# A decoder layer on one core: the first token gather reads two rounded parts of the normed rows, split by ScalarE and GpSimd

## The chip, the cores and the metric

One core of a Trainium2 chip runs the whole program. The time is that of the device for one execution, in microseconds (us); the metric is the median of several. Engines are called as the profile calls them: PE (TensorE, matmuls), PEld (its weight loads), DVE (VectorE), ACT (ScalarE), POOL (GpSimd) and SP (SyncE, which issues nearly all DMAs). "Granted clock" is the share of TensorE's 2.4 GHz that the chip lets through: 1.0 or 0.5 (1.2 GHz).

## The reference, cut to what matters

256 tokens of width 1024 pass one layer: a token mixing part (sparse attention, stick-breaking attention, output projections), a LayerNorm, a router and a mixture of 32 experts, of which each token uses 4. The part that matters here:

```
x  = post_norm(ALPHA * x + gate1 * y, ln1_g, ln1_b)        # 256 x 1024
h  = layer_norm(x) * (1 + scale2) + shift2
logits = h @ w_router + b_router;  top 4 of 32 -> gate
for each expert e: rows of h of its tokens -> gu -> clamped SwiGLU -> down, weighted, summed per token
x  = post_norm(ALPHA * x + gate2 * y, ln2_g, ln2_b)
```

All is float32. The weights of the experts are 384 MB of 2 MB blocks and are read once.

## The kernel before, in words

The 256 tokens lie on 128 partitions in two halves (`tt` is 0 or 1). The program has two parts: token mixing (about the first 256 us) and the experts (the rest). Between them lies a short chain around the router.

**The chain between the parts.** For each half, `normed(tt)` writes the new rows `x`, `logits(tt)` transposes them on PE and multiplies with the router's weights, and `stats2(tt)` takes mean and variance. `unit_rows(tt)` (line 900) writes `zz[:, tt, :]`, the normed rows without scale and shift, with one DVE instruction of 1024 columns. `choose(tt)` (lines 868 to 881) finds the four largest logits, `routed[:, tt, :]` (line 877), and counts on PE how many tokens with the same expert stand ahead (`pspos`). `place(tt)` makes `posm` (line 885) and from it the one-hot matrix `A0` (line 887), two DVE instructions per half, 64 columns each: column p of expert a is 1 where the token is the p-th of expert a. Two experts (`STATIC`) are handled first, with 64 places each, so `A0` is used in 128 columns. All these DVE instructions are pinned to their order in the program: `unit_rows(0)`, `choose(0)`, `unit_rows(1)`, `choose(1)`, `place(0)`, `place(1)`.

**The gather.** `gather(g, kp)` (lines 1083 to 1099) multiplies the normed rows, as stationary operand in blocks of 128x128, with the one-hot matrix of group `g`, as moving operand. The result `psg` is the transposed rows of the group's tokens; ACT applies scale and shift and writes `xt` (line 1098). Group 0 (the two first experts) uses the float32 rows `zz` and a float32 `A0`; the trace has two instructions for each float32 matmul. The later groups (7 of them) use two parts, `zzH` (the rows rounded to fp32r) and `zzL` (what is left), so two matmuls in fp32r. These parts are made by `split_rows` (lines 1279 to 1286): a copy on ACT and a subtraction on DVE for each half, queued on DVE behind the last instruction of `place`.

**The experts.** `plan` lists for each expert four blocks of `w_gu` and two of `w_dn`, 2 MB each. SP issues their loads into a ring of five buffers; a load waits until PE has finished with the block that was in the buffer (`xpump`). PE works in the order of the program: `mult_gu` starts with bias matmuls (`psu<-bgu`, line 1143), then 16 matmuls of 512 columns for each block (line 1149). `after` hangs small jobs behind blocks: `ranking` (the order of the other experts, from line 936 on) behind blocks 0 to 2, and so on.

**What sets the order.** A planner orders each engine's instructions by the program's order and by when its own model thinks them ready; `pin`, `behind` and `issue_after` hold chosen ones in place. Each engine then works strictly in its order.

Of the kernel before, what the change touches and what calls it, by code (L numbers as in the profile page):

```python
# [10 lines left out]
F32 = mybir.dt.float32  # L11
F32R = mybir.dt.float32r
# [7 lines left out]
D = 1024  # L20
# [40 lines left out]
def trunk_kernel(ctx: ExitStack, tc: tile.TileContext, i, out):  # L61
    nc = tc.nc
# [162 lines left out]
    sp = ctx.enter_context(tc.tile_pool(name="sp", bufs=1))  # L225
# [32 lines left out]
    def pin(ins, j=0):  # L258
        if j < 4:
            tc.keep_in_program_order(ins)  # L260
# [144 lines left out]
    biasT = sp.tile([128, HA, S], F32, name="biasT")  # L405
    nc.gpsimd.dma_start(biasT, bass.AP(tensor=fd.tensor, offset=fd.offset, ap=[[1, 128], [384, HA], [1, S]]))
    wukT = sp.tile([128, 4, 128], F32, name="wukT")
# [61 lines left out]
    late = {}  # L469
# [243 lines left out]
    n = 0  # L713
    while units[n][0] in cols:
        conv(n + LA)
        name = units[n][0]
# [63 lines left out]
    zz = sp.tile([128, 2, D], F32, name="zz", tag="gaT")  # L780
# [35 lines left out]
    n = n_mix  # L816
# [14 lines left out]
    m8s, lgs, anchor = [], [], []  # L831
# [3 lines left out]
    def normed(tt):  # L835
        z = zz[:, tt, :]
        residual(tt, 1)
        pin(zbn[tt, 1])
        mv, rs = finish_stats(wk, zst[tt], f"z{tt}", late=True)
        pin(nc.vector.scalar_tensor_tensor(z, z, mv[:, 0:1], l1g, op0=ALU.subtract, op1=ALU.mult))  # L840
        pin(nc.vector.reciprocal(rs, rs))
        pin(nc.vector.scalar_tensor_tensor(x[:, tt, :], z, rs, l1b, op0=ALU.mult, op1=ALU.add))

    def stats2(tt):
        st = wk.tile([128, 2, 6], F32, name=f"st_h{tt}", tag="st", bufs=4)
        for a in range(2):
            pin(nc.vector.bn_stats(st[:, a, :], x[:, tt, a * 512:(a + 1) * 512]))
        ln2[tt] = finish_stats(wk, st, f"h{tt}", late=True)
# [35 lines left out]
    def place(tt, ps):  # L884
        pin(nc.vector.scalar_tensor_tensor(posm[:, tt, :], ps, 1.0, routed[:, tt, :], op0=ALU.add, op1=ALU.mult))
        for a in range(STATIC):
            ins = nc.vector.tensor_scalar(A0[:, tt, a * 64:(a + 1) * 64], iota[:, :64], posm[:, tt, a:a + 1], None,
                                          op0=ALU.is_equal)
            pin(ins)
        return ins  # L890

    A0 = sp.tile([128, 2, 256], F32, name="A", tag="wukT")
    normed(0)
    logits(0)
    normed(1)
# [1 line left out]
    def unit_rows(tt):  # L897
        mv, rs = ln2[tt]
        pin(nc.vector.reciprocal(rs, rs))
        pin(nc.vector.tensor_scalar(zz[:, tt, :], x[:, tt, :], mv[:, 0:1], rs, op0=ALU.subtract, op1=ALU.mult))  # L900

    stats2(0)
    stats2(1)
    unit_rows(0)
    ps = choose(0)
    unit_rows(1)
    ps1 = choose(1)
    place(0, ps)
# [81 lines left out]
    def base_sums(pT4):  # L990
        for tt in range(2):
            for nh in range(2):
                ps = tp.tile([128, 512], F32, name="psbd")
                nc.tensor.matmul(ps, pT4[:, 2 + tt, :], bdn[:, nh * 512:(nh + 1) * 512], start=True, stop=True)
                nc.scalar.copy(acc[:, tt, nh * 512:(nh + 1) * 512], ps)
# [65 lines left out]
    for j in range(STATIC, E):  # L1061
# [5 lines left out]
        used += wide[j]  # L1067
    A, XT, SL, OT, AT, YS, P, PY, ACTV = {0: A0}, {}, {}, {}, {}, {}, {}, {}, {}

    def width(g):  # L1070
        return sum(wide[j] for j in groups[g])
# [10 lines left out]
    def gather(g, kp):  # L1082
        n = width(g)
        if kp == 0:
            XT[g] = sp.tile([128, 8, 256], F32, name="xt", tag="hL" if g % 2 else "qlT")
        ps = ms.tile([128, 2, 256], F32, name="psg")
        for q in range(2):
            k = 2 * kp + q
            ks = slice(k * 128, (k + 1) * 128)
            terms = [(z, tt) for z in ((zz,) if g == 0 else (late["zzH"], late["zzL"])) for tt in range(2)]  # L1090
            for m, (z, tt) in enumerate(terms):
                ins = nc.tensor.matmul(ps[:, q, :n], z[:, tt, ks], A[g][:, tt, :n], start=(m == 0),  # L1092
                                       stop=(m == len(terms) - 1))
                if g:
                    behind(ins, m)
        for q in range(2):
            k = 2 * kp + q
            nc.scalar.activation(XT[g][:, k, :n], ps[:, q, :n], AF.Identity, scale=mc[:, 1, k:k + 1],  # L1098
                                 bias=mc[:, 0, k:k + 1])

    def behind(ins, n):
        tc.keep_in_program_order(ins)

    def slots(j):
        g, c = gof[j]
        for t, m in enumerate(parts_of[j]):
            ps = ms.tile([128, 2], F32, name="pss")
            n = 0
            for tt in range(2):
                for h in range(128 // m):  # L1110
                    hot = A[g].bitcast(F32) if g else A[g]
                    behind(nc.tensor.matmul(ps[m * h:m * h + m, :], hot[:, tt, c + 64 * t:c + 64 * t + m],  # L1112
                                            rouR[:, tt, seq[j], :], start=(tt == 0), stop=(tt == 1),
                                            tile_position=(0, m * h)), n)
                    n += 1
            sl = wk.tile([128, 2], F32, name="sl", tag="slt", bufs=6)
            nc.vector.tensor_copy(sl, ps)  # L1117
            ot = wk.tile([128, S], F32R, name="ot", tag="pT", bufs=4)
            nc.vector.tensor_scalar(ot, iota, sl[:, 0:1], None, op0=ALU.is_equal)
            OT[j, t] = ot  # L1120
            SL[j, t] = sl
# [134 lines left out]
    for g in range(1, len(groups)):  # L1256
        n0 = at_unit[groups[g][0], 0, 0]
        job(max(n0 - 7, 1), one_hot, g)
        for kp in range(4):
            job(n0 - 6 + kp, gather, g, kp)  # L1260
        for j in groups[g]:
            job(at_unit[j, 0, 2], slots, j)
    for j in range(STATIC):
        job(at_unit[j, 0, 3] + 1, slots, j)
    for kp in range(4):
        gather(0, kp)
# [9 lines left out]
    def sorted_rows():  # L1276
        late["pT4"] = ranked()

    def split_rows():
        late["zzH"] = sp.tile([128, 2, D], F32R, name="zzH", tag="biasT")  # L1280
        late["zzL"] = sp.tile([128, 2, D], F32R, name="zzL")
        with tc.issue_after(anchor[2].ins):
            for tt in range(2):
                nc.scalar.copy(late["zzH"][:, tt, :], zz[:, tt, :])
                nc.vector.tensor_sub(late["zzL"][:, tt, :], zz[:, tt, :], late["zzH"][:, tt, :].bitcast(F32))

    acc = sp.tile([128, 2, D], F32, name="acc", tag="hH")
    for n, f in ((0, ranking), (1, ranking), (2, split_rows), (2, ranking), (3, sorted_rows),
                 (5, lambda: base_sums(late["pT4"]))):
        after.setdefault(n, []).insert(0, (f, ()))  # L1290
    xpump()
# [116 lines left out]
```

## Time and profile before

| | |
|---|---|
| median of 3 runs | 1219.64 us (1218.18 to 1220.34) |
| the profiled execution | 1221.51 us, of it 1219.7 us span of instructions |
| busy in the span | PE 86%, PEld 39%, DVE 35%, ACT 19%, POOL 4% |
| mean granted clock | 0.937 |
| DMA | 451.95 MB, 371 GB/s on the mean, 424 GB/s in most slices after 335 us |

The profile is one execution. A time in its timeline counts from the first instruction. Busy shares are means over stages with different limits; the change touches some 15 us around 270 us, so the rows further down are from there, and from places where the same kinds of instructions stand.

### The profile page before, as it was taken

To read this page: it belongs to the slowest core of one execution; us is meant where nothing else is said; L and a number is where in the kernel's file an instruction comes from. 1 tells how busy PE (TensorE), PEld (TensorE's weight loads), DVE (VectorE), ACT (ScalarE), POOL (GpSimd) and SP (SyncE) were. 2 spreads that over 40 slices of the span, in tenths; PEclk is the share of its full clock that TensorE was granted. 3 is DMA by queue.
4 is the path that set the end of the run, shared out by engine and by line. 5 is a ranking of instruction groups with operands and counts; after the bars stand their busy time and mean duration, and the time that the engine had idled before them with its cause. 6 is when DMAs were issued, how large, how long until landed. Compare 5 with 4: busy or idle time off the path is not lost.

```text
span 1219.7 us, 15731 instructions
## 1 busy us (share of the span) xinstructions
PE 1049.6 (86%) x6505; PEld 475.9 (39%) x6505; DVE 421.0 (35%) x810; ACT 233.7 (19%) x435; POOL 46.1 (4%) x93
## 2 busy tenths in 40 slices
PE   5997999989989889988989897989797979779764
PEld 5885878873323232333323222232123213322211
DVE  7788976782112121212121212121212211112234
ACT  2546655431200110011010101020001000100001
POOL 2140201000000000000000000000000000000001
PEclk9998999979999998999899998999899989999886
DMA  9956657377899999999999999999999999979993
GB/s 363 341 200 253 247 207 292 139 271 291 335 424 407 422 424 425 417 424 424 425 417 423 424 425 425 426 425 425 425 425 425 424 425 425 425 313 416 425 423 148
DMA packets 96270, 451.95 MB, mean 371 GB/s; under 512 B 5342, under 2 KB 6558, under 8 KB 64450
## 3 DMA queue, kind: packets, MB, share of 16 engines
q1 hardware_dynamic: 95442, 449.42, 90.5%
q0 software_dynamic: 752, 1.47, 0.4%
q8 instruction: 53, 0.87, 0.3%
q14 instruction: 23, 0.19, 0.0%
HBM read 461.98 MB, written 1.47 MB: 380 GB/s over the span
## 4 chain that ended last, share of the span: by engine, by line
issue 78%; PE 13%; DVE 6%; POOL 1%; ACT 0%; DMA 0%; SPq 0%; POOLq 0%; DVEq 0%; ACTq 0%
PE psp L430 4%; PE psn L449 2%; PE psy L797 2%; PE psbr L767 2%; DVE ada L290 1%; DVE ada L267 1%; DVE WL L214 1%; PE pt L502 1%; PE psr L310 1%; PE psob L679 0%; PE pso L616 0%; DMA w<-in_w_ada_dram 0%; DVE sco L566 0%; DVE m L565 0%; PE psl L597 0%
## 5 line engine op out<-in xcount | busy, mean ns | idle before, releaser
L1149 PE MATMUL psu<-wx,xt 128*64 128x512 f32 (+1 forms) x2432 | 438.4, 624 | 64.2 <-DMA wx<-in_w_gu_dram 64.0
L1165 PE MATMUL psd<-wx,at 128*64 128x512 f32 (+1 forms) x1216 | 248.8, 660 | 44.8 <-DMA wx<-in_w_dn_dram 44.8
L1149 PEld LDWEIGHTS psu<-wx,xt 128*64 128x64 f32 (+1 forms) x2432 | 114.1, 125 | 298.8 <-issue 217.3
L1210 DVE TENSOR_TENSOR acc<-acc,psc 128x512 f32<-128x512 f32 x128 | 82.2, 683 | 215.9 <-PE psc L1206 215.9
L1165 PEld LDWEIGHTS psd<-wx,at 128*64 128x64 f32 (+1 forms) x1216 | 63.8, 133 | 223.8 <-issue 153.2
L1198 DVE SCALAR_TENSOR_TENSOR ys<-psd,sl,ys 128x512 fp32r<-128x512 f32 x36 | 27.0, 751 | 239.3 <-ACT ys L1197 238.9
L1176 ACT ACTIVATE gm<-psu 128x512 f32<-128x512 f32 (+1 forms) x38 | 22.6, 594 | 434.2 <-PE psu L1149 368.5
L1178 DVE TENSOR_SCALAR uc<-psu 128x512 f32<-128x512 f32 (+1 forms) x38 | 26.3, 692 | 148.9 <-PE psu L1149 75.3
L1197 ACT ACTIVATE ys<-psd,sl 128x512 fp32r<-128x512 f32 x36 | 24.7, 687 | 256.2 <-PE psd L1165 220.8
L214 DVE TENSOR_TENSOR WL<-w,WH 128x1024 fp32r<-128x1024 f32 (+1 forms) x52 | 64.4, 1255 | 20.2 <-ACT WH L213 18.4
L430 PE MATMUL psp<-hH,WH 128*128 128x256 f32 x224 | 66.3, 296 | 0.0
L430 PE MATMUL psp<-hH,WL 128*128 128x256 f32 x224 | 63.7, 286 | 2.3 <-DVE WL L214 2.3
L430 PE MATMUL psp<-hL,WH 128*128 128x256 f32 x224 | 63.5, 284 | 0.0
L213 ACT CAST WH<-w 128x1024 fp32r<-128x1024 f32 (+1 forms) x52 | 53.2, 1043 | 40.0 <-PE psp L430 15.0
L1206 PE MATMUL psc<-ys,ot 64*128 64x512 f32 x304 | 54.5, 441 | 1.8 <-ACT ys L1227 0.9
L1098 ACT ACTIVATE xt<-psg,mc 128x256 f32<-128x256 f32 (+2 forms) x64 | 31.1, 536 | 106.5 <-PE psg L1092 106.5
L1206 PEld LDWEIGHTS psc<-ys,ot 64*128 64x128 f32 x304 | 24.4, 187 | 57.4 <-issue 43.6
L267 DVE SCALAR_TENSOR_TENSOR ada<-w,cs,ada 128x512 f32<-128x512 f32 x56 | 45.5, 818 | 1.1
L430 PEld LDWEIGHTS psp<-hH,WH 128*128 128x128 f32 x224 | 43.4, 194 | 3.4 <-issue 3.3
L430 PEld LDWEIGHTS psp<-hH,WL 128*128 128x128 f32 x224 | 43.2, 193 | 2.9 <-DVE WL L214 2.7
L430 PEld LDWEIGHTS psp<-hL,WH 128*128 128x128 f32 x224 | 43.2, 193 | 0.3 <-issue 0.2
L1117 DVE COPY sl<-pss 128x2 f32<-128x2 f32 x38 | 6.0, 159 | 98.2 <-PE pss L1112 97.7
(313 smaller groups left out, 902.1 us busy)
## 6 DMA issues: line engine op xcount, KB each, us to landing
wx<-in_w_gu_dram SPq DMA_DIRECT2D x128, 2048.0 KB, 14.3
wx<-in_w_dn_dram SPq DMA_DIRECT2D x64, 2048.0 KB, 15.3
w<-in_w_in_dram SPq DMA_DIRECT2D x8, 2048.0 KB, 11.4
w<-in_w_ada_dram SPq DMA_DIRECT2D x8, 2048.0 KB, 9.2
w<-in_w_ada_dram SPq DMA_DIRECT2D x8, 1024.0 KB
w<-in_w_o_dram SPq DMA_DIRECT2D x2, 2048.0 KB
w<-in_w_a_out_dram SPq DMA_DIRECT2D x1, 2048.0 KB
w<-in_w_b_out_dram SPq DMA_DIRECT2D x1, 2048.0 KB
```

The lines of the kernel that those rows point to most:

```text
L213: a = nc.scalar.copy(wh, src)
L214: b = nc.vector.tensor_sub(wl, src, wh.bitcast(F32))
L267: pin(nc.vector.scalar_tensor_tensor(a, w[:, k, :], cs[:, k:k + 1], a, op0=ALU.mult, op1=ALU.add), j)
L430: nc.tensor.matmul(pp[b // 2][:, b % 2, :], l[:, q, bs], r[:, k, :], start=(k == 0 and b % 2 == 0 and m == 0), stop=(k == 7 and m == 2), s ...
L1098: nc.scalar.activation(XT[g][:, k, :n], ps[:, q, :n], AF.Identity, scale=mc[:, 1, k:k + 1], bias=mc[:, 0, k:k + 1])
L1149: behind(nc.tensor.matmul(ps[p0:p0 + m, :], XT[g][:, k, c + 64 * t:c + 64 * t + m], w[:, q, c0:c0 + 512], start=False, stop=(k == 7), tile ...
L1165: behind(nc.tensor.matmul(PY[j, t][p0:p0 + m, :], AT[j][:, k, 64 * t:64 * t + m], w[:, q, h * 512:(h + 1) * 512], start=(k == 0 or odd and ...
L1178: nc.vector.tensor_scalar(uc[:n, :], pu, LIMIT + 1.0, 1.0 - LIMIT, op0=ALU.min, op1=ALU.max)
L1197: nc.scalar.activation(ys[:, 0, :], py, AF.Copy, scale=gate)
L1198: nc.vector.scalar_tensor_tensor(ys[:, 1, :], py, gate, ys[:, 0, :].bitcast(F32), op0=ALU.mult, op1=ALU.subtract)
L1206: behind(nc.tensor.matmul(pp[h], OT[j, t][hs, tt * 128:(tt + 1) * 128], YS[j, t][hs, a, :], start=(t == 0 and a == 0), stop=(t == tiles[j] ...
L1210: nc.vector.tensor_add(acc[:, tt, ns], acc[:, tt, ns], pp[h])
```

## The change

`zzH` and `zzL` are made inside `unit_rows`, each half as soon as its rows are written: `zzH` by ACT as before, `zzL` by GpSimd in place of DVE. `A0` becomes fp32r. The first gather uses the same terms as the later ones, in the order (zzH, half 0), (zzH, half 1), (zzL, half 0), (zzL, half 1). `split_rows` goes.

```diff
-    A0 = sp.tile([128, 2, 256], F32, name="A", tag="wukT")
+    A0 = sp.tile([128, 2, 256], F32R, name="A", tag="wukT")
+    zzH = sp.tile([128, 2, D], F32R, name="zzH", tag="biasT")
+    zzL = sp.tile([128, 2, D], F32R, name="zzL")
...
         pin(nc.vector.tensor_scalar(zz[:, tt, :], x[:, tt, :], mv[:, 0:1], rs, op0=ALU.subtract, op1=ALU.mult))
+        nc.scalar.copy(zzH[:, tt, :], zz[:, tt, :])
+        nc.gpsimd.tensor_sub(zzL[:, tt, :], zz[:, tt, :], zzH[:, tt, :].bitcast(F32))
...
-            terms = [(z, tt) for z in ((zz,) if g == 0 else (late["zzH"], late["zzL"])) for tt in range(2)]
+            terms = [(z, tt) for z in (zzH, zzL) for tt in range(2)]
...
-                    hot = A[g].bitcast(F32) if g else A[g]
+                    hot = A[g].bitcast(F32)
...
-    def split_rows():
-        late["zzH"] = sp.tile([128, 2, D], F32R, name="zzH", tag="biasT")
-        late["zzL"] = sp.tile([128, 2, D], F32R, name="zzL")
-        with tc.issue_after(anchor[2].ins):
-            for tt in range(2):
-                nc.scalar.copy(late["zzH"][:, tt, :], zz[:, tt, :])
-                nc.vector.tensor_sub(late["zzL"][:, tt, :], zz[:, tt, :], late["zzH"][:, tt, :].bitcast(F32))
-
...
-    for n, f in ((0, ranking), (1, ranking), (2, split_rows), (2, ranking), (3, sorted_rows),
+    for n, f in ((0, ranking), (1, ranking), (2, ranking), (3, sorted_rows),
```

## Rows read from the trace of the kernel before

**Rows 1.** Stretches: us, busy (count) of PE, PEld, DVE, ACT, POOL, clock, DMA.

```profile
275.00:280.00 5.00, 4.62 (x26) 1.78 (x25) 0.29 (x1) 0.80 (x2) 0.00 (x0) 1.00 0.00 0
310.00:320.00 10.00, 10.00 (x48) 4.88 (x50) 0.00 (x0) 2.62 (x5) 0.00 (x0) 0.83 0.62 220
400.00:800.00 400.00, 357.26 (x2155) 119.81 (x2155) 82.08 (x168) 40.41 (x76) 0.00 (x0) 0.94 1.02 423
```

**Rows 2.** Timeline of SP: start, length, line, operation, tiles, count (later timelines too).

```profile
279.09 8.71 SPq L1052 DMA_DIRECT2D wx<-in_w_gu_dram  x3
```

**Rows 3.** Timeline of PE: the first gather, then the first block of expert weights.

```profile
269.25 5.81 PE L1092 MATMUL psg<-A,zz 128*128 128x128 f32 x32
274.99 0.62 PE L1143 MATMUL psu<-bgu,sel_b 96*64 96x512 bf16 x4
...
278.97 0.63 PE L936 MATMUL pscnt<-routed,ones 128*128 128x32 f32 x4
```

**Rows 4.** Timeline of DVE, ACT and POOL between the rows and the gather.

```profile
265.03 1.04 ACT L1284 CAST zzH<-zz 128x1024 fp32r<-128x1024 f32 x1 [0.82 <-DVE zz L900]
...
265.47 0.20 DVE L872 MAX8 m8r<-lg 128x8 f32<-128x40 f32 x1
...
265.76 0.26 POOL L915 TENSOR_SCALAR nm<-m8r 128x1 f32<-128x1 f32 x1 [54.90 <-DVE m8r L872]
...
266.42 0.81 DVE L900 TENSOR_SCALAR zz<-x,mv_h,rs_h 128x1024 f32<-128x1024 f32 x1
...
268.37 0.18 DVE L877 TENSOR_SCALAR routed<-lr 128x32 f32<-128x32 f32 x1
...
268.68 0.42 DVE L887 TENSOR_SCALAR A<-iota,posm 128x64 f32<-128x64 f32 x2
...
269.28 0.19 DVE L885 SCALAR_TENSOR_TENSOR posm<-pspos,routed 128x32 f32<-128x32 f32 x1 [0.18 <-PE pspos L881]
269.51 0.42 DVE L887 TENSOR_SCALAR A<-iota,posm 128x64 f32<-128x64 f32 x2
...
270.05 1.22 DVE L1285 TENSOR_TENSOR zzL<-zz,zzH 128x1024 fp32r<-128x1024 f32 x1
```

**Rows 5.** Groups by form on POOL: operation, tiles, shapes, count, busy us, mean ns.

```profile
L394 POOL TENSOR_TENSOR b<-b,bt 128x512 f32<-128x512 f32 x2 | 2.3, 1155 | 0.1
```

**Rows 6.** Timeline of DVE and POOL where both read SBUF together, two places.

```profile
64.17 1.15 POOL L394 TENSOR_TENSOR b<-b,bt 128x512 f32<-128x512 f32 x1
...
64.44 1.04 DVE L543 TENSOR_SCALAR sco<-rl,kv 128x256 f32<-128x256 f32 x1
...
148.57 3.43 POOL L592 TENSOR_TENSOR lm<-biasT,ma 128x1024 f32<-128x1024 f32 x1 [0.90 <-PE pt L502]
149.74 3.35 DVE L214 TENSOR_TENSOR WL<-w,WH 128x1024 fp32r<-128x1024 f32 x1
```

**Rows 7.** Timeline of PE: matmuls of few columns, and gathers of later groups.

```profile
262.95 3.62 PE L861 MATMUL psrt<-wm,xT 128*128 128x32 f32 x16
...
803.66 0.39 PE L1092 MATMUL psg<-A,zzL 128*128 128x224 f32 x2
803.89 0.39 PE L1092 MATMUL psg<-A,zzH 128*128 128x224 f32 x2
...
818.91 0.60 PE L1092 MATMUL psg<-A,zzL 128*128 128x224 f32 x2
819.34 0.40 PE L1092 MATMUL psg<-A,zzH 128*128 128x224 f32 x2
```

**Rows 8.** Stretches, PE alone: us, busy (count), granted clock, DMA share, GB/s.

```profile
263.00:266.30 3.30, 3.30 (x17) 0.50 0.93 334
...
269.90:273.20 3.30, 3.30 (x17) 0.50 0.58 236
273.30:276.60 3.30, 3.30 (x25) 1.00 0.00 1
...
290.30:293.60 3.30, 3.30 (x8) 0.50 1.03 432
```

## The prediction

> **What bounds the kernel now.** I read the stretches first, then SP's timeline, then the engines around the gather. From about 335 us on the load of expert weights is the limit: 423 GB/s at a DMA share of 1.02 from 400 to 800 us [rows 1]. Before that it is not: the DMA engines stand still from 275 to 280 us, since all five buffers are full, and are at 0.62 from 310 to 320 us [rows 1]. The stream goes on at 279.09 us, when SP gets the first buffer back [rows 2]; that is when PE ends the first block, just after 278.97 us [rows 3]. So each us by which PE ends the first block earlier or later moves the whole stream of 192 blocks, and with it the end. Ahead of that block stand the bias matmuls at 274.99 us and the first gather, 32 instructions from 269.25 us [rows 3]. What the change does to 274.99 and to 278.97 us is what it does to the time.
>
> **Part by part.** *The matmuls.* Before, 16 float32 matmuls are 32 instructions. After, 2 parts x 2 halves x 8 blocks are again 32, in fp32r. What does one cost? Matmuls of only 32 columns stand at (3.62 - 0.40) / 15 = 0.21 us from each other at the half clock [rows 7], where 0.40 is the length of the last: 32 columns can't take that, so the load of 128x128 weights sets the pace. Is it so for fp32r? The later gathers answer it: 224 columns would stream in 224 / 1.2 GHz = 0.187 us at half and 0.093 us at full clock, but two of them take 0.43 us (818.91 to 819.34) and 0.23 us (803.66 to 803.89) [rows 7], that is 0.213 and 0.113 us each, the same floor. Float32 at 128 columns has it too: 17 of the 32 instructions touch the 3.3 us from 269.9 us at half clock [rows 3, 8]. So the new matmuls cost at least 0.107 (128 columns at 1.2 GHz) and at most 0.213 us at half clock; I take 0.213, which is the nearest row. The change saves nothing per instruction.
>
> The Trainium skill, page "TensorE: Matmul & The Clock Gate", section "Weight-path perf modes — Fast Weight Load (FWL) and DoubleRow", has weights loaded faster where there are 128 of them and the type is not FP32. If fp32r counted as such a type, the gather would pace at its columns. The 224-column rows above speak against it; what it would give is the first rival.
>
> *zzH* costs nothing new: ACT makes it at 265.03 us already, right behind its rows [rows 4].
>
> *zzL on POOL.* DVE took 1.22 us for a half [rows 4]. POOL took 1.155 us for a subtraction of 512 columns [rows 5], which makes 2.31 us for a half of 1024, and 3.43 us for an addition of 1024 with a DVE instruction beside it [rows 6]; I take 2.31, the same operation. The first half starts when zzH is there: 265.03 + 1.04 + 0.09 = 266.16 us, with 0.09 from DVE's end at 265.67 to POOL's start at 265.76 [rows 4]. It ends at 268.47 us.
>
> *What this holds up on DVE.* DVE instructions that read SBUF beside a POOL instruction wait for its end: the tensor_scalar at 64.44 us ended at 65.48, right after POOL's at 65.32; the subtraction of 1024 columns at 149.74 us took 3.35 us and ended 1.09 us after POOL's end at 152.00 [rows 6], against 1.22 us alone [rows 4]. The second half's rows are a tensor_scalar of the same kind as the first of these, due at 266.42 us [rows 4]: 0.26 us after POOL took hold. It waits until 268.47 and ends about 0.73 us later (its 0.81 less some 0.1 that is already under way), at 269.20 instead of 267.23 us: 2.0 us late. Behind it on DVE stand the second half's choice and both halves' one-hots, and PE waits for these. (Bounds: nothing, if it slips in first; 3.1 us with POOL at 3.43.)
>
> zzH of half 1 then ends at 269.20 + 0.04 + 1.04 = 270.28 us, and zzL of half 1 holds POOL from 270.37 to 272.68 us. On DVE the choice needs 1.45 us from the end of the rows to the first one-hot (267.23 to 268.68) [rows 4]: due at 270.65, again inside POOL's hold. So the one-hots start at 272.68: 0.42, then 0.19 + 0.04 for `posm`, then 0.42, all done at 273.75 instead of 269.93 us [rows 4]. If `routed` (due 1.14 us behind the rows, at 270.34) is caught as well, 1.56 us follow POOL's end instead, which is 274.24.
>
> On this the Trainium skill's "GPSIMD Engine Reference", section "Key points", is narrower than my rows: it puts the contention to DVE instructions in a two-port mode or with two SBUF inputs. By it `posm`, with one input from PSUM, would pass, and the sum stays at 273.75; were every DVE instruction held, it would be 274.24.
>
> *The gather.* zzL is there (272.68), so `A0` is what it waits for. Its first half is ready at 273.10, the second at 273.75; I take 273.5 as the start of 32 instructions at 0.213 us: end at 280.3 us. Before, the next instruction started at 274.99. **First term: 5.3 us late.** Of it 3.8 to 4.3 is the wait and the rest the clock: before, the clock rose at about 273.2 us, after 4.0 us of gather with 128-column float32 matmuls (0.50, then 1.00) [rows 8]. From 263.0 to 266.3 us PE had no gap either, but with 32-column matmuls, and the clock stayed at 0.50 [rows 8]. The fp32r matmul streams its columns once where float32 goes through twice the work in the same 0.213 us, so it lies between; I take it that the clock stays at half through the gather.
>
> *The first block.* At full clock it took 278.97 - 274.99 = 3.98 us with its bias matmuls. At half clock it would be 7.96, if the clock never rose; if it had risen, 3.98. The half-clock stretch at 290.3 us, filled with expert matmuls, was over by 293.7 [rows 8], so I take some 3.2 us of half clock here, which lose half of that. **Second term: 1.6 us** (0 to 4).
>
> *What is freed on DVE* (2 x 1.22 us of subtraction) was hidden: it came behind the one-hots, and the next thing that PE needs of DVE comes after 278.97 us. It gains nothing, and costs nothing.
>
> *Later.* The sum is 6.9 us at 279 us, and nothing absorbs it: all loads until 310 us are released by PE. But two stretches of half clock follow, at 290.3 [rows 8] and between 310 and 320 (0.83 of 10 us) [rows 1]; each loses 1.7 us, and each comes after small router matmuls with gaps. Moved in time they may be missed or caught anew: 3.4 us less to 1.7 more. **Third term: I take 1.2 us less.** Together 5.7 us: 1221.51 + 5.7 = 1227.2 us for an execution like the profiled one. That lay 1.87 us over the median of the runs, so I forecast 1219.64 + 5.7 = 1225.3 us.
>
> **The rivals.** *The weights of fp32r load fast* (the rule of the page above), and DVE isn't held. For: none of the rows has fp32r below 224 columns. Against: the 224-column pace. The gather takes 32 x 0.107 = 3.4 instead of 5.7 us, and starts to run through when zzL of half 1 is there, 267.61 + 1.03 (zzH's start before and length) + 0.09 + 2.31 = 271.0 us, 1.1 later than `A0`: 1.2 us less, 1218.4 us, faster than before. It decides as long as the wait stays under 2.3 us.
>
> *DVE isn't held*, the rest as forecast. For: L900 could be served between POOL's reads. Against: all four instants in rows 6. Then zzL at 271.0 us, three matmuls already done, 29 x 0.213 = 6.2: end 277.2, 2.2 us late; with 1.6 and -1.2 that is 1222.2 us.
>
> *The clock rises inside the gather*, 4.0 us after its start as before. For: PE has no gap. Against: the stretch at 263 us. 19 instructions at 0.213 and 13 at 0.111 from 273.5 end at 279.0: 4.0 us, no loss in the block, less 1.2: 1222.4 us.
>
> *The change doesn't do what it says*: the planner could put both subtractions on POOL behind its small instructions for the second half's `choose`, so not "as soon as the rows are there" but from about 268.4 us (the second `routed`). DVE's rows are then not held, zzL is complete at 268.4 + 2 x 2.31 = 273.0 us, and 29 x 0.213 us behind it the gather ends at 279.2: 4.2 + 1.6 - 1.2, 1224.2 us.
>
> **How the numbers follow.** Forecast 0.60 (own range 1222.5 to 1229.4, the upper end with POOL at 3.43 in both halves, 2.2 us more, `routed` held, 0.5 more, and no dip missed: 6.9 + 2.7 = 9.6); clock 0.14; DVE not held 0.12; fast loads 0.08; planner 0.06. A measurement of this kernel tells 0.2% (2.4 us, so 1217.2 to 1222.1) from no change. Of the two rivals at 1222.2 and 1222.4 I put half on each side, of the first one 0.05 beyond the bound (with a dip missed): faster 0.05, same 0.17, slower 0.78. The range 1220.6 to 1229.4 leaves out the fast loads, part of the middle rivals and a longer half clock.
>
> **What would show it.** In the profile after: DVE's L900 of half 1 stretched to over 2 us or started at about 268.5; the second POOL subtraction ending near 272.7; L887 after it; 32 instructions of `psg` at 0.213 us with granted clock 0.50 to the end; the first SP load at 286 us in place of 279.09. Wrong if L887 ends before 271 us, if `psg` paces below 0.2 us at half clock, or if the clock is 1.00 before the expert matmuls.

## The result and the profile after

The changed kernel takes 1225.9 us in the median of 5 runs (1224.36 to 1226.04), the kernel before 1219.64 (1218.07 to 1220.34). The medians lie 6.3 us apart, which is 0.51%; the ratio on record is 1.0061 with a 95% interval of 1.0050 to 1.0072, which would be 7.4 us. Either way the change is slower, clear of the noise. The forecast was 1225.3 us.

In the changed profile (span 1223.9 us, the execution 1225.9) everything ahead of the change lies 0.25 us earlier: the first half's normed rows start at 263.93 instead of 264.18 us. Timeline of DVE, changed kernel, from the second half's rows to the one-hots (start, length, line, operation, tiles, count); the lines answer to [rows 4]:

```profile
266.17 2.66 DVE L902 TENSOR_SCALAR zz<-x,mv_h,rs_h 128x1024 f32<-128x1024 f32 x1
...
269.97 0.18 DVE L877 TENSOR_SCALAR routed<-lr 128x32 f32<-128x32 f32 x1
270.06 0.18 DVE L885 SCALAR_TENSOR_TENSOR posm<-pspos,routed 128x32 f32<-128x32 f32 x1
270.28 2.28 DVE L887 TENSOR_SCALAR A<-iota,posm 128x64 fp32r<-128x64 f32 x2
272.49 0.18 DVE L885 SCALAR_TENSOR_TENSOR posm<-pspos,routed 128x32 f32<-128x32 f32 x1
272.70 0.42 DVE L887 TENSOR_SCALAR A<-iota,posm 128x64 fp32r<-128x64 f32 x2
```

And POOL's, in the same stretch:

```profile
265.90 2.38 POOL L904 TENSOR_TENSOR zzL<-zz,zzH 128x1024 fp32r<-128x1024 f32 x1
...
269.99 2.36 POOL L904 TENSOR_TENSOR zzL<-zz,zzH 128x1024 fp32r<-128x1024 f32 x1 [0.18 <-ACT zzH L903]
```

Read them together: L902 starts at 266.17, inside POOL's first instruction (265.90 to 268.28), and ends at 268.83, 0.55 behind that one's end; it took 0.81 us before. L887 starts at 270.28, inside POOL's second (269.99 to 272.35), and the first pair is over at 272.56. `posm` (L885), which has one input in PSUM, runs through in between, in its usual 0.18 us. The one-hots are ready at 273.12 instead of 269.93 us. Below, "hold" stands for this: a DVE instruction that waits until GpSimd's is over.

PE of the changed kernel at the start and the end of the gather and behind it, to be held against [rows 3]:

```profile
272.71 1.00 PE L1096 MATMUL psg<-A,zzH 128*128 128x128 f32 x3 [1.87 <-DVE posm L885]
...
278.42 0.63 PE L1096 MATMUL psg<-A,zzL 128*128 128x128 f32 x2
278.84 0.63 PE L1096 MATMUL psg<-A,zzH 128*128 128x128 f32 x2
279.27 0.63 PE L1096 MATMUL psg<-A,zzL 128*128 128x128 f32 x2
279.83 1.06 PE L1147 MATMUL psu<-bgu,sel_b 96*64 96x512 bf16 x4
280.68 5.41 PE L1153 MATMUL psu<-wx,xt 128*64 128x512 f32 x16
286.02 0.63 PE L940 MATMUL pscnt<-routed,ones 128*128 128x32 f32 x4
```

The gather starts at 272.71, just behind the first pair of one-hots (272.56); zzL is complete by then (272.35). Two matmuls take 0.42 or 0.43 us from start to start, to the very end of the gather; before, they ran at half of that from 273.2 us on. The first block with its bias matmuls takes 6.19 us (279.83 to 286.02), 3.98 before. The clock says why. PE of the changed kernel by stretches (us, busy and count, granted clock, DMA share, GB/s), against [rows 8]:

```profile
273.30:276.60 3.30, 3.30 (x17) 0.50 0.01 2
276.70:280.00 3.30, 3.30 (x17) 0.50 0.00 0
280.10:283.40 3.30, 3.30 (x12) 0.50 0.00 0
283.50:286.80 3.30, 3.16 (x14) 0.87 0.00 0
310.00:320.00 10.00, 9.32 (x42) 1.00 0.99 367
```

The clock stays at half through the whole gather and rises only in the block. SP's next load comes with it, 7.05 us later than in [rows 2]:

```profile
286.14 8.70 SPq L1056 DMA_DIRECT2D wx<-in_w_gu_dram  x3
```

The last stretch above gives a part back: from 310 to 320 us the clock is 1.00, where it was 0.83 [rows 1].

### The profile page after: what moved, and what is told of

Read it like the earlier page. It is cut to its first block, busy times and chain, and to the rows that moved or that the text cites. A ratio compares the mean times of both kernels' runs of the same rounds, so it can differ in the third digit from the quotient of the medians.

```text
span 1223.9 us, 15733 instructions
## 1 busy us (share of the span) xinstructions
PE 1044.1 (85%) x6505; PEld 473.5 (39%) x6505; DVE 422.7 (35%) x808; ACT 233.7 (19%) x435; POOL 50.7 (4%) x95
## 4 chain that ended last, share of the span: by engine, by line
PE 59%; DMA 32%; DVE 6%; issue 1%; ACT 1%; POOL 1%; POOLq 0%; SPq 0%; DVEq 0%
PE psu L1153 23%; DMA wx<-in_w_dn_dram 22%; PE psd L1169 14%; DMA wx<-in_w_gu_dram 10%; PE psp L430 5%; PE psg L1096 2%; PE psn L449 2%; PE psy L797 2%; PE psc L1210 2%; PE psbr L767 2%; DVE ada L290 1%; PE psu L1147 1%; DVE ada L267 1%; DVE acc L1214 1%; PE pta L1192 1%
## 5 line engine op out<-in xcount | busy, mean ns | idle before, releaser
L1169 PE MATMUL psd<-wx,at 128*64 128x512 f32 (+1 forms) x1216 | 238.6, 637 | 50.6 <-DMA wx<-in_w_dn_dram 50.6
L1169 PEld LDWEIGHTS psd<-wx,at 128*64 128x64 f32 (+1 forms) x1216 | 60.7, 129 | 221.1 <-issue 144.4
```

What stands on the lines that cost most here:

```text
L1169: behind(nc.tensor.matmul(PY[j, t][p0:p0 + m, :], AT[j][:, k, 64 * t:64 * t + m], w[:, q, h * 512:(h + 1) * 512], start=(k == 0 or odd and ...
```

## The experiments

So that shifts from earlier parts of the program drop out, times count from the start of the first half's normed rows (L900 before, L902 or so elsewhere): when the last one-hot is ready, when the gather gives way to the bias matmuls, and when SP issues the first load behind the first block. These three columns are read from the one profiled execution of each kernel. The ratio is that of run times to the kernel before on the same chip, as it stands on record; it is not always the quotient of the two medians. Each experiment has 11 or 12 runs, the one in four pieces 6, the change 5. The row of before has its median on the two chips of the experiments (1218.18 to 1218.26 us); beside the change it took 1219.64.

| kernel | one-hots | gather over | first load | median us | ratio, 95% |
|---|---|---|---|---|---|
| before | 5.75 | 10.81 | 14.91 | 1218.2 | 1 |
| the change | 9.19 | 15.90 | 22.21 | 1225.9 | 1.0061 (1.0050 to 1.0072) |
| GpSimd's subtraction, float32 gather | 9.18 | 14.76 | 18.86 | 1222.58 | 1.0027 (1.0017 to 1.0037) |
| fp32r gather, no GpSimd | 5.75 | 12.45 | 18.65 | 1222.60 | 1.0031 (1.0019 to 1.0042) |
| subtraction on DVE behind the one-hots | 5.74 | 13.95 | 20.75 | 1223.05 | 1.0038 (1.0027 to 1.0048) |
| subtraction in four pieces | 8.18 | 14.89 | 21.20 | 1224.20 | 1.0060 (1.0040 to 1.0079) |
| before, clock kept up | 5.52 | 9.45 | 13.55 | 1217.30 | 0.9991 (0.9978 to 1.0004) |
| the change, clock kept up | 9.19 | 13.19 | 17.29 | 1219.34 | 1.0017 (1.0003 to 1.0031) |
| before, clock kept up, four banks | 5.52 | 8.81 | 12.91 | 1217.64 | 0.9986 (0.9974 to 0.9997) |
| fp32r gather, clock kept up | 5.52 | 11.20 | 16.54 | 1220.71 | 1.0018 (1.0007 to 1.0029) |
| fp32r gather, 256 columns | 5.74 | 11.39 | 15.49 | 1218.93 | 1.0000 (0.9987 to 1.0012) |
| the change, 256 columns | 9.18 | 14.95 | 19.05 | 1222.15 | 1.0029 (1.0015 to 1.0043) |
| fp32r gather, 256 columns, clock kept up | 5.52 | 9.79 | 13.89 | 1217.28 | 0.9990 (0.9977 to 1.0004) |

**The hold alone.** The later groups need zzH and zzL anyway, so GpSimd's work can stay while the first gather reads the float32 rows (and `A0` is float32 again).

```diff
-            terms = [(z, tt) for z in (zzH, zzL) for tt in range(2)]
+            terms = [(z, tt) for z in ((zz,) if g == 0 else (zzH, zzL)) for tt in range(2)]
```

> The subtraction stays on GpSimd as in the change, but the first gather reads the float32 rows zz and a float32 A0 as before, so it doesn't need zzL. Theory 1 (GpSimd holds DVE's instructions, and the half clock adds to it): DVE's L902 of half 1 is still stretched to about 2.7 us, A0 is ready 3.4 us later than before, the gather is as long as before (5.8 us) or shorter by the clock's phase, and the first load after the gather is issued 3 to 5 us later than in the kernel before (measured from the start of the first L900/L902: 14.9 us there); time 1222 to 1224 us. Rival (the loss is the wait for zzL, the rest follows from it): nothing waits for zzL, so 1219.6 us.

Measured: L902 is 2.65 us long, the one-hots are as late as in the changed kernel, the first load comes 3.95 us later than before, and the time is 0.27% up. DVE, POOL and PE of this kernel:

```profile
266.30 2.36 POOL L904 TENSOR_TENSOR zzL<-zz,zzH 128x1024 fp32r<-128x1024 f32 x1
...
266.57 2.65 DVE L902 TENSOR_SCALAR zz<-x,mv_h,rs_h 128x1024 f32<-128x1024 f32 x1
...
273.10 6.05 PE L1096 MATMUL psg<-A,zz 128*128 128x128 f32 x32 [1.87 <-DVE posm L885]
```

Nothing in this gather reads zzL, so the rival that the loss is the wait for it falls: GpSimd's instructions cost time by what they hold up on DVE.

**The kind of matmul alone.** DVE makes zzL late as before the change, and the gather reads zzH twice.

```diff
-        nc.gpsimd.tensor_sub(zzL[:, tt, :], zz[:, tt, :], zzH[:, tt, :].bitcast(F32))
...
+            terms = [(z, tt) for z in ((zzH, zzH) if g == 0 else (zzH, zzL)) for tt in range(2)]
```

> No subtraction on GpSimd: DVE makes zzL late, as before the change. The first gather reads zzH twice in place of zzH and zzL (it leaves out the low part for the two first experts), in fp32r. No hold and no wait for zzL, only the other kind of matmul. Theory 1: A0 is ready as before, 32 matmuls pace at 0.213 us with granted clock 0.50 to their end (6.8 us, against 5.8 before), and the first block of expert weights runs partly at half clock: first load 2 to 4 us later, time 1221 to 1223 us. Rival (the wait for zzL is the loss): 1219.6 us or below. Rival (fp32r weights load fast): the pace is about 0.107 us and the time 1217 to 1218 us.

Measured: one-hots as before, first load 3.74 us later, 0.31% up. The pace is (6.63 - 0.41) / 29 = 0.214 us, with 0.41 for the length of the last one, and it lasts to the end, all of it at half clock:

```profile
269.68 6.63 PE L1095 MATMUL psg<-A,zzH 128*128 128x128 f32 x30 [0.17 <-DVE ex L927]
...
276.24 1.06 PE L1146 MATMUL psu<-bgu,sel_b 96*64 96x512 bf16 x4
...
277.10 5.29 PE L1152 MATMUL psu<-wx,xt 128*64 128x512 f32 x16
```

```profile
269.70:276.20 6.50, 6.50 (x30) 0.50 0.24 94
```

fp32r weights don't load faster. The two parts of the change, alone, add up as far as the intervals of about 0.1% on each side can tell: 0.27 + 0.31 = 0.58%, against 0.61% together (0.51% by the medians); 3.95 + 3.74 = 7.7 us at the first load, against 7.3.

**The wait in place of the hold.** DVE subtracts, pinned right behind the last one-hot.

```diff
     placed = place(1, ps1)
+    for tt in range(2):
+        pin(nc.vector.tensor_sub(zzL[:, tt, :], zz[:, tt, :], zzH[:, tt, :].bitcast(F32)))
```

> The change, but DVE makes zzL, both halves right behind the last one-hot; GpSimd holds nothing. Theory 1: L902 of half 1 takes 0.81 us, A0 is ready as in the kernel before, zzL is complete 2.45 us after it; the gather then runs at 0.213 us to its end: about 3.6 us later than before, with the half clock in the first block 5 to 6 us at the first load; after missed or caught dips 1223 to 1225 us. So most of the loss stays although the hold is gone: hold and wait cover each other. Rival (the hold is the loss): 1220 to 1221 us.

Measured: the hold is gone (one-hots at 5.74 us), but the gather now waits for zzL, 0.38 and 0.45 us at two places, and goes on at half clock:

```profile
269.55 0.69 PE L1097 MATMUL psg<-A,zzL 128*128 128x128 f32 x2 [0.38 <-DVE zzL L914]
270.69 0.47 PE L1097 MATMUL psg<-A,zzL 128*128 128x128 f32 x1 [0.45 <-DVE zzL L914]
```

The first load is 1.5 us earlier than in the changed kernel, no more, and the ratio is 1.0038. GpSimd's hold and the wait for zzL hide each other; taking one away leaves the other and the clock.

**How long a hold lasts.** GpSimd's subtraction in four instructions of 256 columns.

```diff
-        nc.gpsimd.tensor_sub(zzL[:, tt, :], zz[:, tt, :], zzH[:, tt, :].bitcast(F32))
+        for c in range(4):
+            cs_ = slice(c * 256, (c + 1) * 256)
+            nc.gpsimd.tensor_sub(zzL[:, tt, cs_], zz[:, tt, cs_], zzH[:, tt, cs_].bitcast(F32))
```

> The change, but GpSimd's subtraction of each half is cut into four instructions of 256 columns (about 0.6 us each). Theory 1, if a hold lasts one GpSimd instruction and DVE comes in between two: L902 of half 1 ends at most 0.6 us late plus its own 0.81, so about 1.4 us long and not 2.7; the second zzL still ends late, so the first load comes 20 to 21 us after the start of the first L902 (22.2 in the changed kernel, 14.9 before) and the time is 1 to 2 us below the changed kernel's. Rival, if the two engines only share the rate of reading: L902 of half 1 is as long as in the changed kernel, 2.6 us, and the time is the same as there.

POOL and DVE of this kernel:

```profile
264.22 3.25 POOL L906 TENSOR_TENSOR zzL<-zz,zzH 128x256 fp32r<-128x256 f32 x4
...
264.48 1.03 DVE L902 TENSOR_SCALAR zz<-x,mv_h,rs_h 128x1024 f32<-128x1024 f32 x1
...
267.63 1.42 DVE L887 TENSOR_SCALAR A<-iota,posm 128x64 fp32r<-128x64 f32 x2
```

L902 is 1.03 us long instead of 2.66, and POOL's four pieces take 3.25 us instead of 2.38: the engines take turns, instruction by instruction. A shared rate of reading would have left L902 as long as before. The other half of the expectation failed: the first load comes only 1.0 us earlier (21.20), since each pair of one-hots now waits for a piece (1.42 and 1.23 us instead of 0.42), and `routed` too (0.66 us instead of 0.18); the ratio, 1.0060, can't be told from the changed kernel's.

**The clock by itself.** Matmuls that compute nothing (a constant of 256 columns into a bank that is free) fill PE's idle time ahead of the gather.

```diff
+            tc.keep_in_program_order(nc.tensor.matmul(dum, ident, iota, start=True, stop=True))
```

With 11 of them in the kernel before:

> The kernel before, with matmuls added that compute nothing (256 columns of a constant, 11 of them) in PE's idle time between the normed rows and the gather. Theory 1 (the clock at half is a cost of its own here): the granted clock is 1.00 through most of 258 to 275 us, the gather's 32 float32 instructions pace at 0.111 us from their first to their last (3.6 us against 5.8), the first load is issued about 2 us earlier, time 1217 to 1218.5 us, faster than both kernels. Rival (the clock of the gather is hidden, the first load or the stream waits for something else): 1219.6 us. Rival (the added matmuls stand in the way): slower, up to 1222 us.

With more of them in the changed kernel (20; the expectation below says 22):

> The changed kernel with the added matmuls that compute nothing (22 of 256 columns) ahead of the gather, in PE's idle time. The hold stays as it is. Theory 1 (hold and clock are separate terms): A0 ready as in the changed kernel, the granted clock 1.00 in the gather, its pace 0.111 us between waits for ACT, 4 to 4.5 us in all instead of 7.1, the first block 4.0 instead of 6.3 us: the first load about 17.5 us after the start of the first L902 (22.2 without), time about 4 us below the changed kernel's, 0.1 to 0.3% over the kernel before. Rival (fp32r matmuls of 128 columns are slow in themselves): the gather stays near 7 us at full clock.

Measured: in the kernel before, the first load comes 1.36 us earlier, less than the 2 expected, because the gather at full clock has to wait for ACT to empty PSUM banks; the ratio's interval just includes 1. The wait:

```profile
275.80 2.05 PE L1101 MATMUL psg<-A,zz 128*128 128x128 f32 x16 [0.29 <-ACT xt L1107]
```

In the changed kernel the first load comes 4.9 us earlier, at 17.29 us (17.5 expected), and the time falls from 1.0061 to 1.0017. Its gather at full clock, by stretches of PE:

```profile
272.10:276.40 4.30, 3.97 (x32) 1.00 0.01 4
```

So here fp32r matmuls of 128 columns keep a full clock for 4.3 us; the miss below must be held against that.

**Four banks.** The stall for ACT taken away as well:

```diff
-        ps = ms.tile([128, 2, 256], F32, name="psg")
+        ps = (mm if g == 0 and kp % 2 else ms).tile([128, 2, 256], F32, name="psg")
```

> The kernel before with the 11 added matmuls, and the four blocks of the first gather in four PSUM banks instead of two in turn. With the added matmuls alone PE waited 0.3 and some 0.2 us in the gather for ACT to empty a bank, and the gather took 4.4 us. Theory 1: 3.7 to 3.9 us now, first load 12.9 to 13.1 us after the start of the first L900 (13.55 without the banks, 14.91 before), time 1216 to 1217.5 us where the kernel before has 1218.3, the fastest of all. Rival (nothing here reaches the end): as the kernel before.

Measured: first load at 12.91 us, as expected; the ratio is 0.9986 (0.9974 to 0.9997), the median 1217.64 us where 1216 to 1217.5 was expected. It is the one kernel whose interval lies below 1, if barely, and it beats the changed kernel clearly. That it is the fastest of all isn't shown: the kernels at 0.9990 and 0.9991 can't be told from it. Its gather takes 3.81 us:

```profile
268.68 3.81 PE L1101 MATMUL psg<-A,zz 128*128 128x128 f32 x32 [0.23 <-DVE posm L894]
```

**fp32r with the clock up, a miss.**

> The gather in fp32r from zzH twice (leaves the low part out for the two first experts; zzL made late by DVE), with the 11 added matmuls. Theory 1 (fp32r costs time here only through the clock): the pace at full clock is 0.111 us as for float32, the first load comes 13.5 us after the start of the first L902, as with the added matmuls and float32, and the 3.7 us that fp32r cost at half clock are gone; time 1217 to 1218.5 us. Rival (the load of fp32r weights is quicker at full clock): pace below 0.09 us, first load below 13 us. Rival (fp32r is slow in itself): first load at 16 us or later.

First load at 16.54 us, not 13.5. The rivals fall too: the load is no quicker, and "16 us or later" came, but not because fp32r is slow in itself, since the pace at full clock was 0.11 us in the changed kernel with the clock kept up. PE by timeline and by stretches shows what happened:

```profile
268.26 0.41 PE L889 MATMUL pspos<-routed,before 128*128 128x32 f32 x2 [0.75 <-DVE routed L885]
268.90 0.41 PE L1104 MATMUL psg<-A,zzH 128*128 128x128 f32 x2 [0.23 <-DVE posm L894]
269.49 5.60 PE L1104 MATMUL psg<-A,zzH 128*128 128x128 f32 x30 [0.19 <-DVE ex L936]
```

```profile
268.90:270.70 1.80, 1.61 (x13) 1.00 1.02 412
270.80:274.90 4.10, 4.10 (x20) 0.50 0.17 70
```

The gather began at full clock, and the clock fell inside it at 270.7 us, after 1.2 us in which PE had no gap. Ahead of that PE had stood idle for 0.75, 0.23 and 0.19 us. The float32 gather with four banks had the first two of these gaps as well (0.74 and 0.23 us) and kept the clock. So fp32r costs here not just because the clock was down: a gather with 128 columns of it could not keep the clock up at this place. That it always loses it is not so: in the changed kernel with 20 added matmuls, the last of which end 0.3 us ahead of the gather, matmuls of the same kind kept 1.00. What decides between the two was not tried by itself.

**Twice the columns.** If the load of the weights sets the pace, and the clock rose in the kernel before under float32 matmuls that stream more in the same 0.213 us, then 128 more columns of zeros should cost nothing and bring the clock back. That float32 streams more is read from the added matmuls, float32 of 256 columns at full clock: (3.27 - 0.38) / 13 = 0.22 us each, with 0.38 for the length of the last one, where fp32r matmuls of 256 columns take (278.55 - 278.08) / 4 = 0.12, in the second kernel of this paragraph.

```profile
265.76 3.27 PE L854 MATMUL dum<-iota,ident 128*128 128x256 f32 x14
```

```profile
278.08 0.40 PE L1098 MATMUL psg<-A,zzL 128*128 128x256 f32 x2
278.31 0.40 PE L1098 MATMUL psg<-A,zzH 128*128 128x256 f32 x2
278.55 0.40 PE L1098 MATMUL psg<-A,zzL 128*128 128x256 f32 x2
```

```diff
+    nc.gpsimd.tensor_scalar_mul(A0[:, :, 128:], iota[:, None, :128].to_broadcast([128, 2, 128]), 0.0)
...
-                ins = nc.tensor.matmul(ps[:, q, :n], z[:, tt, ks], A[g][:, tt, :n], start=(m == 0),
+                nw = n if g else 256
+                ins = nc.tensor.matmul(ps[:, q, :nw], z[:, tt, ks], A[g][:, tt, :nw], start=(m == 0),
```

> The fp32r gather from zzH twice without GpSimd's subtraction (the low part left out for the two first experts), but over all 256 columns of A0, of which the upper 128 are zero and unused: twice the columns for nothing. Theory 1 (weights set the pace, and a matmul that streams half of the time lets the clock stay at half): the pace at half clock stays 0.213 us, the clock now rises inside the gather, about 4 us after its start, as with float32 before; the gather takes 5.8 to 6 us instead of 7.4, the first block 4.0 us, so the first load comes 15 to 15.5 us after the start of the first L902 instead of 18.65 with 128 columns; time about 1219 to 1220 us, faster than with half of the work. Rival (matmul work sets the time): 128 more columns cost up to 0.1 us each at half clock, first load at 18.7 us or later.

> The changed kernel whole, GpSimd's subtraction and both parts, with the first gather over 256 columns of which the upper 128 are zero. Theory 1: the hold stays (A0 9.2 us after the start of the first L902), the clock rises inside the gather, the first load comes at 18.8 to 19.5 us instead of 22.2: what stays is the hold alone, as with float32 rows and the hold (18.86); time 1222 to 1223 us, 3 us below the changed kernel. Rival (matmul work sets the time): 22 us or later.

> The fp32r gather from zzH twice over 256 columns, with the 11 added matmuls ahead. With 128 columns the clock fell inside the gather, 1.8 us after its start, and the first load came at 16.54 us. Theory 1: with 256 columns it doesn't fall, the pace is 0.119 us throughout and the first load comes at 13.7 to 14 us, as with float32 (13.55); time 1217 to 1218.5 us. Rival (the fall belongs to fp32r or to the place): 16.5 us again.

All three first loads came as expected (15.49, 19.05 and 13.89 us), the times too, within 0.1 us. The first gather took 6.3 us where 5.8 to 6 was expected. PE of the first of the three, by timeline and by stretches:

```profile
267.87 6.39 PE L1097 MATMUL psg<-A,zzH 128*128 128x256 f32 x32
```

```profile
267.90:272.60 4.70, 4.64 (x20) 0.50 0.58 230
272.80:276.00 3.20, 3.20 (x25) 1.00 0.00 0
```

With twice the columns the gather is over 1.06 us earlier, the first load comes 3.16 us earlier (15.49 instead of 18.65) and the time is that of the kernel before. In the changed kernel the same zeros take 3.16 us off as well, and what is left, 1.0029, is that of the hold alone (1.0027). With the clock kept up, 256 columns keep it where 128 lost it, with the same gaps ahead (0.74 and 0.23 us):

```profile
268.00:272.70 4.70, 4.43 (x32) 1.00 0.61 234
```

## Why the prediction was right, point by point

*Bound.* The end moved with the first block, as said. The thirteen kernels of the table show it: a straight line through their ratios rises by 0.08%, 1.0 us, for each us of the first load, and none lies more than 0.1% off it. In the two profiles the loss is 7.3 us at the first load and 64.01 - 58.30 = 5.7 us at the first matmul of the down projection, counted as in the table; the two executions differ by 4.4 us, of which the one before was itself 1.9 us over its median.

*zzL on POOL:* 2.31 us forecast, 2.38 and 2.36 measured. The first one started at 266.15 and ended at 268.53 us on the clock of the kernel before (0.25 added), 266.16 and 268.47 forecast.

*The hold on DVE:* the second half's rows were to end at 269.20; they ended at 269.08 (268.83 + 0.25). The one-hots were forecast for 273.75 and came at 273.37 (273.12 + 0.25). `routed` was not caught, which was luck: it started 0.02 us ahead of POOL, and in the kernel with four pieces it was. That every DVE instruction which reads SBUF waits, as the prediction put it, is too wide: `posm` reads `routed` from SBUF and one input from PSUM, and ran through. The experiments with the hold alone and with four pieces bear out the mechanism and that it lasts one instruction.

*Nothing saved per matmul:* 0.213 us each, shown with and without the hold. One of the three rows behind it proves less than it was taken for: float32 of 128 columns, at half of the 0.22 us that 256 columns take at full clock, streams for about as long as its weights load.

*The gather's end:* 280.3 forecast, 280.08 measured. *The first block:* a loss of 1.6 us forecast, 2.2 measured (6.19 - 3.98): the term was a little small, because the half clock lasted to 284.3 us, 4.5 us into the block and not 3.2.

*Later.* 1.2 us less forecast, a guess between 3.4 less and 1.7 more. From the first load to the first matmul of the down projection the changed kernel takes 41.80 us and the kernel before 43.39: 1.6 less. Before there were two stretches at half clock there, at 290.3 and between 310 and 320; now one, at 298 (0.50 from 298.0 to 301.3 us). In the kernel that has none, the change with the clock kept up, the same way takes 40.09 us. Why a stretch falls where it does was not tried by itself. That the guess came so near, and the total with it (5.7 us forecast, 6.3 measured), is in part luck; the terms before it are not.

*The rivals.* Fast fp32r loads and a DVE that isn't held are refuted by the runs above. That the clock rises inside an fp32r gather that starts at half clock is true of 256 columns and false of 128. The planner put the subtractions where the change has them. One slip in the sums: 6.9 + 2.7 us over 1219.64 is 1229.2, not 1229.4, which changes nothing.

What the forecast had not seen is that the clock can also fall inside such a gather, and that the part of the cost that is the clock's can be undone by streaming zeros.

## What to carry to other kernels

Before moving an elementwise instruction to GpSimd, look at which DVE instructions will run beside it: here a tensor_scalar from SBUF to SBUF (2.66 us instead of 0.81), and in the kernel before a subtraction of two SBUF inputs (3.35 instead of 1.22 [rows 6]), waited until GpSimd's whole instruction was over, and on a chain of small DVE instructions that costs more than the DVE time it was to save. A matmul form that streams less is no gain where the load of its weights sets the pace, and here it also left the clock at half; take the pace from a row with the same weights before counting on the columns. When two costs overlap, undo each alone and both: here 0.27% and 0.31% stood side by side, while taking away one wait showed only the next.

## What the runs showed of the hardware that was not expected

More columns made a stretch faster: 32 matmuls of 128x128 fp32r weights took 7.4 us from first start to the next instruction with 128 columns (12.45 - 5.07) and 6.3 with 256 (11.39 - 5.06), at the same 0.213 us each at half clock, since with the wider ones the clock rose to 1.00 at 272.7 us, and with 128 columns it did not. A PE without gaps did not raise it either: in the changed kernel it was busy without a break from 273.3 us on, and the clock stayed at 0.50 to the end of the gather at 279.8. And where the clock had been kept up, fp32r matmuls of 128 columns lost it once, 1.8 us after they began (at 270.7 us), and kept it once, over 4.3 us (272.1 to 276.4 us in the changed kernel with 20 added matmuls).
